# Hybrid decoder step: all row tiles of the down projection in the seven products, results by halves of the columns

## The chip, the cores and the metric

The kernel runs on one core of one Trainium2 chip. Its time is the device time of one execution in microseconds; the verdict compares it with the kernel before, run on the same chip. TensorE (PE, with PEld for its weight loads) multiplies, VectorE (DVE) and ScalarE (ACT) work element by element, GpSimd (POOL) issues some transfers and does a few additions, SyncE (SP) issues most transfers.

## The reference

One step of a two-layer decoder with 1024 prompt tokens and 8 sample tokens, 1032 columns in all, model width 1024 and MLP width 4096, in float32. Layer 0 mixes with gated linear attention, layer 1 with sliding-window attention; both attend to 256 memory tokens. What matters here is the MLP that ends each layer:

```python
def squared_relu_mlp(h, w_up, w_down):
    return jnp.square(jax.nn.relu(h @ w_up)) @ w_down

        f = squared_relu_mlp(rmsnorm(x, norm_ffn_pre[l]), w_ffn_up[l], w_ffn_down[l])
        x = x + rmsnorm(f, norm_ffn_post[l])
```

After layer 0, `x` is normalised again and goes through the K/V and query projections of layer 1. After layer 1, `x` is the output `yT`.

## The kernel before, in words

Activations lie with features on the 128 partitions and tokens in the columns. The 1032 columns are cut into three chunks `CH` of 384, 384 and 264. Every float32 product is made of three matmuls in a reduced type: each operand is split into a high part (a cast on ScalarE, L155) and a low part (a subtraction on VectorE, L156), and high x high, high x low and low x high are summed in PSUM.

The MLP's two projections are done as 2 x 2 block products with seven multiplications in place of eight (the Winograd form of Strassen's scheme). For the down projection the blocks are halves of the output features, halves of the MLP rows and halves of the columns (`HALF` = 516, worked in two parts of `SUB` = 258). The 32 row tiles of the MLP width are cut in two: the first four (`NPL`) are kept out of the scheme and done plainly, the other 28 go in pairs (`PAIRS`) through the seven products, with seven steps `jj` of four row tiles in each.

In the down projection `phases` lists the 49 steps (product, jj) in the order `ORDER` = 1, 7, 6, 5, 2, 3, 4. For each step `load_w` and `load_a` fetch the raw weights (`wr`) and the raw combined activations (`ra`, from the scratch tensor `awd`; three buffers), `prep` forms the product's combination and splits both, and `phase` issues 48 matmuls on eight PSUM banks. `prep` runs two steps ahead into three slots `sas` for the activations and three for the weights. With a product's last step `evict` adds the banks into the four quarter results `acc[11]`, `acc[12]`, `acc[21]`, `acc[22]`, as that product needs. Meanwhile in layer 0 `fold` multiplies layer 1's weights by a gain on GpSimd.

Then `down_plain` does the four plain row tiles chunk by chunk (96 matmuls each, L990 to L992), adds the quarter results to them (L996, L1000) into a tile `F`, and hands each pair of output tiles to `Residual`: squares and sums (`Stats`), a matmul with a constant matrix `ones` that averages over the partitions (L201), the inverse root by Ln and Exp with one Newton step (L208 to L212), then `f * rf`, the gain, the addition of the residual `xd`, and either the store of `xd` and the split for layer 1 (layer 0) or the store of `yT` (layer 1, L323 to L327). `measure` makes the statistics of the new `x`. A number given as `behind` puts the ones-matmul that many matmul columns later in TensorE's order. A scheduler orders each engine's instructions by priority and data; each engine and each queue then runs its list in order.

## Time and profile before

| | us |
|---|---|
| Median of 3 runs (2180.78 to 2186.23) | 2183.07 |
| The profiled execution, its own time | 2190.3 |
| Its span from first to last instruction | 2188.5 |
| TensorE busy in the span | 2143.8 (98%) |
| VectorE / ScalarE / GpSimd busy | 1492.9 / 1054.5 / 117.0 |
| Mean granted clock of TensorE | 0.993 |

The profile is of one execution; its times are used for the parts of the kernel, and differences are carried over to the median. A matmul's duration on the page covers its pipeline, so two neighbours overlap, and the pace is read from their starts. PE counts as busy when a matmul is in flight. On the other engines, an instruction's idle time before it is put down to what released it.

### The profile page before, as it was taken

To read this page: it belongs to the slowest core of one execution; us is meant where nothing else is said; L and a number is where in the kernel's file an instruction comes from. 1 tells how busy PE (TensorE), PEld (TensorE's weight loads), DVE (VectorE), ACT (ScalarE), POOL (GpSimd) and SP (SyncE) were. 2 spreads that over 40 slices of the span, in tenths; PEclk is the share of its full clock that TensorE was granted. 3 is DMA by queue.
4 is the path that set the end of the run, shared out by engine and by line. 5 is a ranking of instruction groups with operands and counts; after the bars stand their busy time and mean duration, and the time that the engine had idled before them with its cause. 6 is when DMAs were issued, how large, how long until landed. Compare 5 with 4: busy or idle time off the path is not lost.

```text
span 2188.5 us, 41306 instructions
## 1 busy us (share of the span) xinstructions
PE 2143.8 (98%) x16814; PEld 2047.8 (94%) x16814; DVE 1492.9 (68%) x2809; ACT 1054.5 (48%) x2095; POOL 117.0 (5%) x128
## 2 busy tenths in 40 slices
PE   8999999999999999999999999899999999999997
PEld 6879999899999999999999878599999999999996
DVE  7556647768877777657569455647887776856557
ACT  6355536557545544333424454646654554433334
POOL 0012000000000002520000000200000000000000
PEclk9999999999999999999999999899999999999998
DMA  5422026543653359474234200424364337635422
GB/s 169 143 67 77 24 65 169 154 136 103 194 174 135 134 199 360 165 262 135 93 94 148 91 19 24 164 89 135 117 213 160 137 132 274 213 110 172 150 89 78
DMA packets 122307, 304.73 MB, mean 139 GB/s; under 512 B 11065, under 2 KB 40817, under 8 KB 121761
## 3 DMA queue, kind: packets, MB, share of 16 engines
q1 hardware_dynamic: 109056, 258.80, 36.0%
q0 software_dynamic: 7728, 30.42, 4.0%
q10 hardware_dynamic: 5328, 12.81, 1.5%
q8 instruction: 134, 2.20, 0.4%
q14 instruction: 61, 0.50, 0.1%
HBM read 213.57 MB, written 89.51 MB: 138 GB/s over the span
## 4 chain that ended last, share of the span: by engine, by line
PE 90%; DVE 4%; ACT 3%; DMA 2%; issue 1%; SPq 0%; DVEq 0%; ACTq 0%
PE mm L251 17%; PE mx L251 8%; PE mx L760 6%; PE mx L762 6%; PE mx L761 6%; PE mx L925 4%; PE mx L927 4%; PE mx L926 4%; PE mm L762 3%; PE mm L760 3%; PE mm L761 3%; PE mm L925 2%; PE mm L926 2%; PE mm L927 2%; PE sx L925 1%; PE sf L926 1%
## 5 line engine op out<-in xcount | busy, mean ns | idle before, releaser
L155 ACT CAST wh<-ws 128x512 fp32r<-128x512 f32 (+1 forms) x262 | 188.3, 726 | 313.8 <-DVE ws L609 100.1
L760 PE MATMUL mx<-xf,wh 128*128 128x258 f32 x1048 | 296.9, 283 | 0.0
L762 PE MATMUL mx<-xf,wl 128*128 128x258 f32 x1048 | 295.7, 282 | 0.0
L761 PE MATMUL mx<-xf,wh 128*128 128x258 f32 x1048 | 295.5, 282 | 0.0
L156 DVE TENSOR_TENSOR wl<-ws,wh 128x512 fp32r<-128x512 f32 (+1 forms) x262 | 213.5, 821 | 105.2 <-ACT wh L155 103.9
L251 PE MATMUL mm<-xh,wh 128*128 128x384 f32 (+1 forms) x864 | 282.2, 327 | 0.5 <-ACT xh L155 0.4
L251 PE MATMUL mm<-xh,wl 128*128 128x384 f32 (+1 forms) x864 | 279.2, 323 | 0.0
L251 PE MATMUL mm<-xl,wh 128*128 128x384 f32 (+1 forms) x864 | 278.3, 322 | 0.0
L155 ACT CAST wh<-wr 128x1024 fp32r<-128x1024 f32 x98 | 103.0, 1051 | 319.3 <-PE sx L926 303.7
L156 DVE TENSOR_TENSOR wl<-wr,wh 128x1024 fp32r<-128x1024 f32 x98 | 119.8, 1223 | 175.9 <-ACT wh L155 175.9
L925 PE MATMUL mx<-sa,wh 128*128 128x258 f32 x784 | 221.2, 283 | 0.0
L926 PE MATMUL mx<-sa,wh 128*128 128x258 f32 x784 | 220.5, 281 | 0.0
L927 PE MATMUL mx<-sa,wl 128*128 128x258 f32 x784 | 220.4, 281 | 0.0
L761 PEld LDWEIGHTS mx<-xf,wh 128*128 128x128 f32 x1048 | 198.0, 189 | 0.4
L760 PEld LDWEIGHTS mx<-xf,wh 128*128 128x128 f32 x1048 | 197.6, 189 | 0.4
L762 PEld LDWEIGHTS mx<-xf,wl 128*128 128x128 f32 x1048 | 197.8, 189 | 0.0
L251 PEld LDWEIGHTS mm<-xh,wh 128*128 128x128 f32 x864 | 162.9, 189 | 10.4 <-issue 7.0
L251 PEld LDWEIGHTS mm<-xl,wh 128*128 128x128 f32 x864 | 162.9, 189 | 7.2 <-issue 6.3
L251 PEld LDWEIGHTS mm<-xh,wl 128*128 128x128 f32 x864 | 162.5, 188 | 6.8 <-issue 4.9
L926 PEld LDWEIGHTS mx<-sa,wh 128*128 128x128 f32 x784 | 148.3, 189 | 0.0
L927 PEld LDWEIGHTS mx<-sa,wl 128*128 128x128 f32 x784 | 148.0, 189 | 0.0
L925 PEld LDWEIGHTS mx<-sa,wh 128*128 128x128 f32 x784 | 147.4, 188 | 0.1
(560 smaller groups left out, 5782.8 us busy)
## 6 DMA issues: line engine op xcount, KB each, us to landing
ra<-awd SPq DMA_DIRECT2D x98, 516.0 KB, 3.6
ws<-in_w_up SPq DMA_DIRECT2D x64, 512.0 KB, 5.1
wr<-in_w_downb SPq DMA_DIRECT2D x56, 512.0 KB, 4.9
awd<-aw SPq DMA_DIRECT2D x26, 1032.0 KB, 6.7
awd<-am SPq DMA_DIRECT2D x28, 774.0 KB, 8.3
ws<-in_w_in_a SPq DMA_DIRECT2D x20, 512.0 KB, 3.9
xd<-f ACTq DMA_DIRECT2D x24, 384.0 KB, 4.7
ws<-in_w_out SPq DMA_DIRECT2D x16, 512.0 KB, 3.6
```

Of the source, the lines that this page charges most:

```text
L155: nc.scalar.copy(hi, src)
L156: (eng or nc.vector).tensor_tensor(lo, src, f32(hi), ALU.subtract)
L251: mm = nc.tensor.matmul(ps[:M, :n], w_[:, k, :M], x_[:, k, :], start=(i == 0), stop=(i == 3 * KT - 1))
L760: nc.tensor.matmul(ps, wh(k), xh, start=(k == 0), stop=False)
L761: nc.tensor.matmul(ps, wh(k), xl, start=False, stop=False)
L762: mm = nc.tensor.matmul(ps, wl(k), xh, start=False, stop=(k == n - 1))
L925: nc.tensor.matmul(ps, wh[:, q, ms], h, start=(jj == 0 and q == 0), stop=False)
L926: nc.tensor.matmul(ps, wh[:, q, ms], lo, start=False, stop=False)
L927: mm = nc.tensor.matmul(ps, wl[:, q, ms], h, start=False, stop=end)
```

## The change

The plain stage is gone. `NJ` = 8 steps in place of seven: the four plain row tiles of the up projection are still computed plainly, but now `plain_factors` forms their combinations in the up stage (eight subtractions or additions on VectorE, with loads and stores), and they enter the seven products as the step jj = 7. Three of the factors are read straight from `apd`. The order of the products becomes `DOWN` = 1, 7, 6, 4, 2, 5, 3, so that `acc[11]` and `acc[21]`, the left half of the columns, are complete after the fifth product, and `acc[22]` after the sixth; the seventh adds only to `acc[12]`.

The seventh product is done in two passes `s` over the two parts of 258 columns, 16 steps of 24 matmuls, with four banks in each pass. Its eight weight splits are kept for the second pass (`lasting`). The raw activations have two buffers in place of three, the halves of a fold take a temporary tile `t3`.

The result is not put together by chunks any more. `Closing` works on four pieces in place: `pa` (chunk 0, left columns 0 to 384), `pb` (132 columns of chunk 2), `pc` (258 columns of chunk 1) and `pd` (the other 126 of chunk 1 and the other 132 of chunk 2). `hook` places their steps among the phases: the squares of piece a four steps before the seventh product, the rest of pieces a and b from that product's start on, piece c in its second pass, and piece d after its end. The gain is multiplied on ScalarE for both layers. In layer 1 the residuals are fetched on GpSimd's queue into rooms of their own; in layer 0 they pass through `t3` on SP's queue.

The core of the diff (the eviction's rule by product, the pools and the tags of tiles are left out):

```diff
+DOWN = (1, 7, 6, 4, 2, 5, 3)
+NJ = DFF // P // 4
...
+        def plain_factors():
+            for q in range(2):
+                rows = [tp.tile([P, 768], F32, tag=tag, name=nm("c"))[:, :HALF] for tag in ("t3", "t3", "tq", "tq")]
+                for r, (m, h) in zip(rows, ((0, 0), (0, 1), (1, 0), (1, 1))):
+                    nc.sync.dma_start(r, apd[l, :, 2 * q + m, h, :])
+                c11, c12, c21, c22 = rows
+                for f_, r, a, b, op in ((1, c12, c22, c12, ALU.subtract), (4, c11, c12, c11, ALU.add),
+                                        (6, c21, c11, c21, ALU.subtract), (5, c22, c22, c11, ALU.subtract)):
+                    yield
+                    TT(r, a, b, op)
...
-        phases = [(p, jj) for p in range(7) for jj in range(NJ)]
+        phases = [(p, jj, None) for p in range(6) for jj in range(NJ)]
+        phases += [(6, jj, s) for s in range(2) for jj in range(NJ)]
+        N = len(phases)
...
-        rap = pool(st2, "left", "ra", 3)
+        rap = pool(st2, "left", "ra", 2)
...
+            order = [(q, mp) for q in range(2) for mp in range(4)]
+            if s is not None:
+                order.sort(key=lambda x: x[1])
+            for q, mp in order:
+                for x, (o, w) in enumerate(cols):
+                    ps = kept["ps"][len(cols) * mp + x][:, :w]
+                    ms = slice(P * mp, P * mp + P)
+                    a = 0 if s else o
+                    h, lo = sa[:, 0, q, a : a + w], sa[:, 1, q, a : a + w]
+                    end = jj == NJ - 1 and q == 1
+                    nc.tensor.matmul(ps, wh[:, q, ms], h, start=(jj == 0 and q == 0), stop=False)
+                    nc.tensor.matmul(ps, wh[:, q, ms], lo, start=False, stop=False)
+                    mm = nc.tensor.matmul(ps, wl[:, q, ms], h, start=False, stop=end)
+                    tick(mm, 3 * w)
+                    kept["mm"] = mm.ins.name
+                    if end:
+                        with first() if s is None else urgent(2):
+                            gather(DOWN[p], ps, *(acc[k][:, mp, o : o + w] for k in (11, 12, 21, 22)))
...
+        pa = piece(early, slice(0, 384), "sf", (0, 0, 384))
+        pb = piece(early, slice(384, HALF), "sx", (2, 0, 132))
+        pc = piece(late_, slice(0, SUB), "sf", (1, 0, SUB))
+        pd = piece(late_, slice(SUB, HALF), "sx", (1, SUB, 384 - SUB), (2, 132, 132))
...
+        def hook(v):
+            if -8 <= v < -4:
+                split(*lasting(v + 8), reg(3, v + 8))
+            if v == -4:
+                pa.feed(0, 1, 2, 3)
+            if v == 0:
+                rooms((pa, "xh0"), (pc, "xl0"))
+                pa.factor(rp.tile([P, 384], F32, tag="rf", name=nm("rf")), 0.3 * unit)
+            if v == 1:
+                pb.feed(0, 1, 2, 3)
+                pb.factor(rx, 2 * unit)
+            if v == 2:
+                pa.close(behind=kept["mm"])
+            if v == 4 and not l:
+                hl[0] = xtiles(0)
+                pa.cut(hl)
+            if v == 5:
+                rooms((pb, "xl2"))
+                pb.close(behind=kept["mm"])
+            if v == 7:
+                pc.feed(2, 3, 0, 1)
+                pc.factor(rb, 1.8 * unit)
+            if v == 9:
+                pc.close((2, 3, 0, 1), behind=kept["mm"])
+            if v == 11:
+                rooms((pd, "xh2"))
+            if v == 10 and not l:
+                rt[0] = rtile(0)
+                pa.measure(0, rt[0], 2.3 * unit, Ring())
+            if v == 11 and not l:
+                hl[1] = xtiles(1)
+                pc.cut(hl)
+                hl[2] = xtiles(2)
+                pb.cut(hl)
...
-        folds = dict(zip((21, 23, 25, 27, 35, 36, 38, 40, 41, 43, 45, 46), (2, 3, 0, 1, 10, 11, 4, 5, 6, 7, 8, 9)))
+        folds = dict(zip((2, 3, 4, 5, 6, 25, 26, 27, 28, 29, 36, 38), (2, 3, 0, 1, 10, 11, 4, 5, 6, 7, 8, 9)))
...
+        if l:
+            with urgent(2):
+                pd.finale()
+                pd.factor(rp.tile([P, 384], F32, tag="rf", name=nm("rf"))[:, : pd.n], 0)
+            pd.close()
```

The steps of `Closing`, which are new:

```python
        def feed(self, *pairs):
            for j in pairs:
                self.sf.add(self.f[:, 2 * j : 2 * j + 2, :])
                self.gain(2 * j, 2 * j + 1)
...
        def factor(self, rf, behind):
            self.rf = rf.unsqueeze(1).to_broadcast([P, 2, self.n])
            self.sf.finish(rf, behind)
...
            for i, j in enumerate(order):
                ks = slice(2 * j, 2 * j + 2)
                xs, fk = got[i], f[:, ks, :]
                TT(fk, fk, self.rf, ALU.mult)
                TT(fk, fk, xs, ALU.add)
...
        def cut(self, hl, order=(0, 1, 2, 3)):
            for j in order:
                ks = slice(2 * j, 2 * j + 2)
                for a, c, at in self.segs:
                    split(hl[c][0][:, ks, at], hl[c][1][:, ks, at], self.f[:, ks, :][:, :, a])
```

Three places show how the order moves. First, VectorE in the last product of layer 0. Before, these are the splits of weights (`wl<-wr`) and activations (`sa<-ra`) for the last steps, then those of the plain stage (`ah`, and `wl<-ws`):

```order
L156 TENSOR_TENSOR wl_10708<-wr_11431,wh_10707 128x1024
L156 TENSOR_TENSOR sa_10702<-ra_13329,sa_10702 128x1032
L156 TENSOR_TENSOR ah_13699<-t_1557_13700,ah_13699 128x768
L156 TENSOR_TENSOR ah_13699<-t_1558_13704,ah_13699 128x768
L156 TENSOR_TENSOR wl_10704<-wr_11616,wh_10703 128x1024
L156 TENSOR_TENSOR sa_10699<-ra_13383,sa_10699 128x1032
L156 TENSOR_TENSOR wl_13558<-ws_13555,wh_13557 128x1024
L156 TENSOR_TENSOR wl_13564<-ws_13561,wh_13563 128x1024
```

Now, in the first pass, the closing of piece a (`acc_10716` and `acc_10717`, with the factor `rf` and the residual tiles `t`), its cut (`xl<-acc`) and piece b's factor (`rx`) stand between the splits of the operands:

```order
L215 SCALAR_TENSOR_TENSOR rf_13696<-sf_13698,rf_13696 128x384
L158 TENSOR_TENSOR sa_10734<-ra_13761,sa_10734 128x2x258
L380 TENSOR_TENSOR acc_10716<-acc_10716,rf_13696 128x2x384 x2
L381 TENSOR_TENSOR acc_10716<-acc_10716,t_1572_13791 128x2x384
L158 TENSOR_TENSOR sa_10732<-ra_13811,sa_10732 128x2x258
L381 TENSOR_TENSOR acc_10716<-acc_10716,t_1573_13793 128x2x384
L380 TENSOR_TENSOR acc_10717<-acc_10717,rf_13696 128x2x384 x2
L158 TENSOR_TENSOR sa_10733<-ra_13841,sa_10733 128x2x258
L381 TENSOR_TENSOR acc_10717<-acc_10717,t_1574_13798 128x2x384
L213 TENSOR_TENSOR sx_13754<-sx_13754,rx_10742 128x132
L158 TENSOR_TENSOR xl_13872<-acc_10716,xh_13871 128x768
L214 SCALAR_TENSOR_TENSOR sx_13754<-sx_13754,rx_10742 128x132
```

A split of 2 x 258 elements is followed by two to five instructions of a piece before the next split comes.

Second, SP's queue in the same product. Before, it holds the loads of the activations, and those of the plain stage's factors (`t<-apd`):

```order
L878 DMA ra_13030<-awd 128x1032
L878 DMA ra_13085<-awd 128x1032
L967 DMA t_1557_13700<-apd 128x2x384
L967 DMA t_1558_13704<-apd 128x2x384
L878 DMA ra_13143<-awd 128x1032
```

Now the residual loads of pieces a, b and c (`t<-xd`) stand between the operand loads:

```order
L975 DMA ra_13881<-awd 128x2x258
L371 DMA t_1575_13803<-xd_94 128x768
L975 DMA ra_13931<-awd 128x2x258
L371 DMA t_1581_13911<-xd_96 128x2x132
L371 DMA t_1582_13913<-xd_96 128x2x132
L975 DMA ra_13959<-awd 128x2x258
L975 DMA ra_14019<-awd 128x2x258
L975 DMA ra_14051<-awd 128x2x258
L371 DMA t_1583_13918<-xd_96 128x2x132
L371 DMA t_1584_13923<-xd_96 128x2x132
L975 DMA ra_14099<-awd 128x2x258
L371 DMA t_1598_14079<-xd_95 128x2x258
```

What moved is the residual: before, its loads (`xs<-xd`) stood behind all operand loads.

Third, VectorE at the end of the program, in layer 1. Before, the statistics of chunk 2 (`f_24917`, factor `rf_25396`) and the closing of chunk 1 (`f_24913`, factor `rf_25229`) alternate:

```order
L1000 TENSOR_TENSOR f_24917<-mx_25378,acc_22020 128x132
L326 TENSOR_TENSOR f_24913<-f_24913,xall_25238 128x768
L323 TENSOR_TENSOR f_24913<-f_24913,rf_25229 128x768 x2
L210 TENSOR_TENSOR sf_25398<-sf_25398,rf_25396 128x264
L326 TENSOR_TENSOR f_24913<-f_24913,xall_25238 128x768
L211 SCALAR_TENSOR_TENSOR sf_25398<-sf_25398,rf_25396 128x264
L323 TENSOR_TENSOR f_24913<-f_24913,rf_25229 128x768
L212 SCALAR_TENSOR_TENSOR rf_25396<-sf_25398,rf_25396 128x264
L323 TENSOR_TENSOR f_24917<-f_24917,rf_25396 128x528 x2
L326 TENSOR_TENSOR f_24917<-f_24917,xall_25407 128x528 x2
L323 TENSOR_TENSOR f_24917<-f_24917,rf_25396 128x528 x2
```

Now the last addition of piece c (`xall_25145`) is followed by the last pass's evictions (L1031), and behind these stands piece d alone (factor `rf_25720`):

```order
L381 TENSOR_TENSOR acc_22258<-acc_22258,xall_25145 128x2x258
L1031 TENSOR_TENSOR acc_22258<-mm_25456,acc_22258 128x258
L1031 TENSOR_TENSOR acc_22258<-mm_25457,acc_22258 128x258
L1031 TENSOR_TENSOR acc_22258<-mx_25458,acc_22258 128x258
L192 TENSOR_TENSOR tq_25698<-tq_25698,tq_25709 128x516
L1031 TENSOR_TENSOR acc_22258<-mx_25459,acc_22258 128x258
L198 TENSOR_TENSOR rf_25720<-tq_25698 128x258
L213 TENSOR_TENSOR sx_25722<-sx_25722,rf_25720 128x258
L214 SCALAR_TENSOR_TENSOR sx_25722<-sx_25722,rf_25720 128x258
L215 SCALAR_TENSOR_TENSOR rf_25720<-sx_25722,rf_25720 128x258
L380 TENSOR_TENSOR acc_22258<-acc_22258,rf_25720 128x2x258 x2
L381 TENSOR_TENSOR acc_22258<-acc_22258,xall_25580 128x2x258 x2
```

No instruction of another piece is left between the factor's Newton steps (L213 to L215) and the last additions.

More of the change, by code (lines that the diff above doesn't have):

```diff
@@ L272, in feed @@
         def feed(self, m):
[L273 to L285 removed]
+            if m % 2:
@@ L315, in load @@
                 got.append(xs)
-            ahead = 4 if self.last else 2
-            for j in range(ahead):
-                load(j)
+            load(0)
+            load(1)
             for j in range(4):
@@ L342, in finish @@
-            return None if self.last else (hl, self.r)
-        def measure(self, behind, pool=None):
-            sx = Stats(self.n, "sx", pool)
-            for j in range(4):
-                sx.add(self.f[:, 2 * j : 2 * j + 2, :])
-            sx.finish(self.r, behind)
+                for k in (2 * j, 2 * j + 1):
+                    g = gains[:, self.gnext, k : k + 1]
+                    nc.scalar.mul(hl[0][:, k, :], f[:, k, :], g)
+                    STT(hl[1][:, k, :], f[:, k, :], g, f32(hl[0][:, k, :]), ALU.mult, ALU.subtract)
@@ L833, in mlp @@
                 square_mean(j - 2)
+            if i == ORDER[3] and j >= 5:
+                next(plain, None)
             if i == ORDER[-1]:
@@ L913, in phase @@
         def phase(t):
[L914 removed]
+            p, jj, s = phases[t]
+            cols = columns(t)
             wh, wl, sa = ready.pop(t)
             if jj == 0:
[L917 to L931 removed]
```

367 lines of the change are left out of this document (204 added, 163 removed).

## The prediction

> **What bounds the kernel now.** I read the page first, for the engine that carries the chain, then a table of windows over the MLP stages, then the timeline of TensorE for the pace of each shape, and last the end of the program.
>
> ```profile
> PE 2143.8 (98%) x16814; PEld 2047.8 (94%) x16814; DVE 1492.9 (68%) x2809; ACT 1054.5 (48%) x2095; POOL 117.0 (5%) x128
> PE 90%; DVE 4%; ACT 3%; DMA 2%; issue 1%; SPq 0%; DVEq 0%; ACTq 0%
> 540.00:822.00 282.00, 282.00 (x2349) 281.40 (x2348) 218.89 (x444) 144.84 (x259) 0.00 (x0) 1.00 0.49 167
> 822.00:1104.00 282.00, 282.00 (x2357) 281.97 (x2355) 181.99 (x199) 106.19 (x113) 62.69 (x36) 1.00 0.59 203
> 1104.00:1150.00 46.00, 46.00 (x295) 45.73 (x294) 34.78 (x65) 14.66 (x20) 0.00 (x0) 1.00 0.24 65
> 1150.00:1160.00 10.00, 10.00 (x59) 9.73 (x58) 9.88 (x15) 8.39 (x12) 0.00 (x0) 1.00 0.64 208
> 1842.00:2125.00 283.00, 283.00 (x2364) 282.96 (x2363) 176.25 (x201) 106.52 (x114) 6.37 (x12) 1.00 0.49 165
> 2125.00:2171.00 46.00, 46.00 (x291) 45.24 (x290) 32.85 (x62) 23.73 (x40) 0.00 (x0) 1.00 0.10 35
> 2171.00:2189.00 18.00, 1.85 (x7) 0.95 (x6) 13.57 (x18) 2.31 (x6) 4.09 (x2) 0.66 0.42 148
> ```
>
> The columns are the window, its length, the busy time of PE, PEld, DVE, ACT and POOL, the granted clock, the DMA share and GB/s. TensorE is 90% of the chain and has no idle time in the up stage (540 to 822), the seven down products (822 to 1104, 1842 to 2125), the plain stage (46 us in each layer) or the start of layer 1. The clock is 1.00 there. So a change inside these stages is worth what it does to the sum of matmul times, as long as the other engines stay ahead; after 2171 us TensorE is done and a tail of 17.5 us runs on VectorE.
>
> **The change part by part.** *Matmul time.* The plain stage issues 4 row tiles x 8 output tiles x 3 terms = 96 matmuls for each of three column chunks (384, 384, 264). It is replaced by an eighth step in each of seven products: 7 x 48 = 336 matmuls of 258 columns. The durations on the page overlap, so I take the pace from starts.
>
> ```profile
> L925 PE MATMUL mx<-sa,wh x392: 277/282/375, 822.5 to 1102.4; 128*128 128x258 f32 x196
> 1104.24 0.34 PE L990 MATMUL mm<-ah,wx 128*128 128x384 f32 x1
> 1127.81 0.33 PE L990 MATMUL mm<-ah,wx 128*128 128x384 f32 x1
> 1138.21 0.28 PE L990 MATMUL mx<-ah,wx 128*128 128x264 f32 x1
> 1148.50 0.28 PE L990 MATMUL mm<-ah,wx 128*128 128x264 f32 x1
> ```
>
> The products run from 822.5 to 1104.24: 7 x 7 x 48 = 2352 matmuls, 119.8 ns each. From 1127.81 to 1138.21 stand five output tiles of 12, 173 ns each at 384 columns; from there to 1148.50 seven of 12, 122.5 ns at 264. Plain: 192 x 0.1733 + 96 x 0.1225 = 45.0 us. New: 336 x 0.1198 = 40.3 us. That is -4.8 us a layer, **-9.6 us**. The two passes of the last product issue the same matmuls in another order. Each layer has one to four more small ones-matmuls for the statistics, since pieces are more than chunks: +0.3 us.
>
> Against it speaks a rule of the Trainium skill, Perfetto Trace Analysis, section Identifying the Most-Contended Engine: headroom on TensorE is judged by weight-load busy time. PEld is full in both stages, so by that rule time would follow the number of loads, 336 against 288. The starts above decide it for columns: two shapes, the same load, 119.8 against 173 ns.
>
> *The tail.* In layer 1 the last chunk's statistics share VectorE and GpSimd with chunk 1's closing.
>
> ```profile
> 2171.13 0.49 DVE L1000 TENSOR_TENSOR f<-mx,acc 128x132 f32<-128x132 f32 x2 [0.20 <-PE mx L992]
> 2173.31 0.42 ACT L209 ACTIVATE rf<-rf 128x264 f32<-128x264 f32 x1
> 2174.15 0.43 DVE L210 TENSOR_TENSOR sf<-sf,rf 128x264 f32<-128x264 f32 x1
> 2174.49 2.21 DVE L326 TENSOR_TENSOR f<-f,xall 128x768 f32<-128x768 f32 x1
> 2176.97 0.94 DVE L323 TENSOR_TENSOR f<-f,rf 128x768 f32<-128x768 f32 x1
> 2177.84 0.42 DVE L212 SCALAR_TENSOR_TENSOR rf<-sf,rf 128x264 f32<-128x264 f32 x1
> 2178.04 1.80 POOL L326 TENSOR_TENSOR f<-f,xall 128x768 f32<-128x768 f32 x1 [2.15 <-issue]
> 2178.29 2.74 DVE L323 TENSOR_TENSOR f<-f,rf 128x528 f32<-128x528 f32 x2
> 2180.95 1.31 DVE L326 TENSOR_TENSOR f<-f,xall 128x528 f32<-128x528 f32 x2
> L327 SPq DMA_DIRECT2D out_yT<-f x12: 372/372/378, 2152.5 to 2184.8; - x12
> out_yT<-f SPq DMA_DIRECT2D x4, 264.0 KB, 2.2
> ```
>
> After the change nothing else is queued there: the order has piece c closed before the last evictions, and no GpSimd add. The Exp ends at 2173.73; three dependent Newton steps of 0.45 (2177.84 to 2178.29) end at 2175.1 in place of 2178.29, -3.2. The first pair of multiplications took 2.66 to the next start beside GpSimd, a pair without it 1.31, -1.4. The last piece goes out in two DMAs a pair of rows, one more issue of 0.37. Tail: **-4.2 us**; bounds 0 (piece c still in line) and -4.6 (the issue hidden). One rule speaks against: the Trainium skill, DMA: Bandwidth & Descriptors, section Specifications, has transfers under 512 B as read-modify-write. The stores of 126 columns have rows of 504 B. No run here shows that price; if it doubled the landing, the tail would gain 2.0 instead.
>
> *VectorE in the last product.* This is the term I trust least. The closing of pieces a, b and c moves between the operand splits on which TensorE waits, and a pass step has only 24 matmuls, 2.88 us.
>
> ```profile
> L598 DVE TENSOR_TENSOR acc<-acc,sx 128x258 f32<-128x258 f32 x1 | 0.4, 424 | 0.0
> L156 DVE TENSOR_TENSOR ah<-t,ah 128x528 fp32r<-128x528 f32 x2 | 1.3, 703 | 0.2 <-ACT ah L155 0.2
> L189 DVE TENSOR_TENSOR tq<-tq,tq 128x768 f32<-128x768 f32 x6 | 5.7, 952 | 2.7 <-ACT tq L183 2.7
> L156 DVE TENSOR_TENSOR wl<-wr,wh 128x1024 fp32r<-128x1024 f32 x2 | 2.5, 1225 | 5.0 <-ACT wh L155 5.0
> 943.00 0.41 DVE L588 TENSOR_TENSOR acc<-mx,acc 128x258 f32<-128x258 f32 x1
> 943.33 0.41 DVE L589 TENSOR_TENSOR acc<-mx,acc 128x258 f32<-128x258 f32 x1
> ```
>
> In layer 0, counted in the order from the sixth product's first eviction to the last split: 20 evictions and 22 other small operations at 0.424, 14 operand splits and 11 operations of 516 columns at 0.70, one weight split of 1.2, 15 operations of 768 columns (closing, cutting and measuring piece a) at 0.952. Sum 50.8 us. Back to back each starts 0.08 before the last one's end (943.00 to 943.33), 83 x 0.08 = 6.6, so 44.2. Available: 2.5 us before the product's end and 15 steps, 45.7. Layer 1 has no cut and no measure, 37.7. So layer 0 fits with 1.5 us to spare, while it also waits for ScalarE and for TensorE's slots; I take +2 there and +0.5 in layer 1, bounds 0 and 7. Two in-order queues are part of that: layer 0's residual stores stand on ScalarE's queue and wait for VectorE's additions, with the casts of the next operands behind them; the residual loads stand on SP's queue and wait for a temporary tile that an addition frees, with the operand loads behind them. In the order each of these waits is for work that stands ahead of the split that the blocked load or cast serves, so I give them no term of their own.
>
> *The join of the layers.* Plain stage and first projections ran with VectorE at 9.88 of 10 us and TensorE never idle. Piece d now ends with TensorE and must be normalised and cut while chunk 0's six projections run: 6 x 24 x 0.1733 = 25.0 us. VectorE's list from the last eviction to the last cut sums to 26.5 us by the same durations, some 22 overlapped. Chunk 1's first matmul is due at about 26.7 us with the transposes and ones-matmuls. +1, bounds 0 and 6.
>
> *What I cost at nothing.* The eight combinations of the plain rows in the up stage (8 x 0.70 us) lie under 282 us of TensorE with VectorE at 218.89; without cover 5.6 us a layer. The folds run by halves on GpSimd:
>
> ```profile
> L240 POOL TENSOR_TENSOR wf<-wf,gains 128x1024 f32<-128x1024 f32 x12 | 49.1, 4094 | 65.0 <-DMA wf<-in_w_in_b 37.1 <-DMA wf<-in_w_kv 27.8
> ```
>
> Their products are needed 200 us later, and five now fall into the first product, where DMA is busiest. Two raw buffers in place of three matter only where loads are slow; that is a rival.
>
> **Sum**: -9.6 - 4.2 + 0.3 + 2.5 + 1.0 = -10.0 us. The profiled execution took 2190.3 us (span 2188.5), 7.2 above the median of the runs, and would take 2180.3; on the median of 2183.07 that is **2173.1 us**. About 0.3% (6.5 us) is what a measurement here can tell from no change.
>
> **The rivals.**
>
> *Loads bound the last product (slower).* With two raw buffers a load is issued only when the split two steps before is done.
>
> ```profile
> ra<-awd SPq DMA_DIRECT2D x7, 516.0 KB, 6.4
> ra<-awd SPq DMA_DIRECT2D x9, 516.0 KB, 3.6
> L155 ACT CAST ah<-t 128x528 fp32r<-128x528 f32 x2 | 1.2, 628 | 0.0
> 815.00:860.00 45.00, 45.00 (x379) 45.00 (x378) 32.09 (x31) 21.62 (x25) 8.73 (x8) 1.00 0.98 366
> ```
>
> The cycle is issue 0.37 + landing + cast 0.63 + split 0.70 for two steps of TensorE, 5.75 us: it decides from a landing of 4.05 us on. At 3.6 us (900 to 950, half busy) it is hidden; at the 6.4 us of 815 to 860, where DMA is 98% busy, each pair of steps loses 2.35, eight pairs 18.8, less some 4.3 of lead: 14.5 a layer. 2173.1 - 2.5 + 29 = **2200 us**. For it: residual loads, stores and layer 1's weights pass the same queue between these loads. Against: 16 operand loads of 258 KB, three residual pieces in and out (774 columns, 3.2 MB each way) and five weight tiles of 512 KB are 13 MB in 46 us, 285 GB/s, under the 366 of that window, and each load is half as large. Slower by 0.3% needs a landing of 5.7. 11%.
>
> *VectorE bounds the last product.* If its operations do not overlap (50.8 against 45.7, 5.1) and it stands idle once for a chain of Square, ones-matmul, Ln and Exp (from 2171.6 to 2173.7 in the tail, 2.1), 7.2 in place of 2.5: **2178 us**, no change. For it: the list is in order, and each chain of a piece leaves the engine and comes back. Against: most chains have splits and other pieces' work queued in between. 12%.
>
> *Chunk 1 waits for piece d.* The order lets piece d's sums wait for the evictions of chunk 0's projections, so its list cannot run ahead of TensorE; 26.5 us without overlap, the chain of 2.1 and a last load of 3.6 behind weights on SP, less 26.7, is 5.5, the whole bound of 6 in place of 1: **2178 us**, no change. Against: before, VectorE was as full there and nothing waited. 7%.
>
> *Weight loads set the pace.* PEld is full in every stage (281.97 of 282, 45.73 of 46). If the number of loads counted, 45.0 x 336/288 = 52.5, +7.5 a layer in place of -4.8: 2173.1 + 24.6 = **2198 us**. The starts of 119.8 and 173 ns behind one and the same load refute it. It is also what the rule on weight-load time would make of the change. 2%.
>
> **How the numbers follow.** Forecast 68%, all of it faster. The second and third rival, 19%, are within 0.3%; the first and fourth, 13%, slower. The range takes in the forecast's bounds, from no stalls and the scatter of the runs (2.7 below their median), 2173.1 - 3.5 - 0.4 - 2.2 = 2167, to the two middle rivals with scatter, 2182. It leaves out the slow rivals and little else.
>
> **What would show it.** Right: each layer's seven products take some 322 us (2688 x 0.1198) and TensorE is idle in them for under 3 us; layer 1's projections start directly behind; from the last matmul to the end pass 13 us, with VectorE's Newton steps back to back. Wrong: TensorE waiting for the operand splits step after step in the last product (VectorE named: second rival; DMA named, landings over 4 us: first), or for the cut at chunk 1 of layer 1's first projections.

## The result, and the profile after

The changed kernel took 2213.26 us (median of 4 runs, 2209.3 to 2217.6) against 2184.52 for the kernel before (2180.78 to 2186.23, on the same chip): the ratio is 1.0134, 95% interval 1.0122 to 1.0146. It is slower by 28.7 us, where 10 us less were forecast. The profiled execution took 2217.6 us, span 2215.8.

The parts of the span, from the first matmul of the seven up products to the first of the down products, from there to the last down matmul, and so on (differences of the first and last starts at those lines, each from one profiled execution):

| us | up, layer 0 | down, layer 0 | attention, layer 1 | up, layer 1 | down, layer 1 | after the last matmul |
|---|---|---|---|---|---|---|
| before | 283.4 | 327.3 | 409.5 | 283.4 | 328.1 | 17.7 |
| after | 307.8 | 330.5 | 411.5 | 286.3 | 328.7 | 14.4 |

The largest loss, 24.4 us, lies in layer 0's up stage, where the prediction had costed everything at nothing. The down stages, which should have won 2.5 and 4 us, won nothing. Only the tail came out on the forecast's side. From the page of after, the busy shares and the chain; TensorE fell from 90% of the chain to 61%, and loads of `ws` stand on it now:

```profile
PE 2144.0 (97%) x16918; PEld 2042.9 (92%) x16918; DVE 1505.1 (68%) x2839; ACT 1083.0 (49%) x2191; POOL 111.4 (5%) x170
PE 61%; DVE 16%; DMA 13%; ACT 6%; issue 4%; SPq 0%; ACTq 0%; POOL 0%; DVEq 0%
```

The windows of after that answer to the first two shown of before (same columns):

```profile
540.00:822.00 282.00, 265.54 (x2154) 260.89 (x2153) 212.11 (x415) 127.67 (x230) 54.17 (x72) 0.99 0.63 203
844.00:1124.00 280.00, 277.30 (x2300) 276.17 (x2301) 182.84 (x200) 120.11 (x142) 0.00 (x0) 0.99 0.48 157
```

TensorE did 2154 matmuls in 282 us where it had done 2349. GpSimd, idle in the up stage before, is busy for 54.17 us there and not at all in the down products: the folds run in the wrong stage. GpSimd's timeline of after shows the first of them:

```profile
645.69 0.58 POOL L244 DMA_DIRECT2D t<-in_w_kv  x1 [306.34 <-ACT aw L851]
...
652.06 1.05 POOL L246 TENSOR_TENSOR t<-t,gains 128x512 f32<-128x512 f32 x1
653.41 0.59 POOL L247 DMA_DIRECT2D wfd<-t  x1 [0.30 <-POOL t L246]
```

The fold's load starts when ScalarE has done with the temporary tile (`aw L851`), over 200 us before the matmul behind which it was put. TensorE's waits in that stage (line waited for: us, times, longest):

```profile
PE mx L818 <- DVE aw L647: 9.5, 8, 2.3
PE mm L818 <- DVE aw L647: 4.0, 3, 3.5
PE mm L818 <- DVE aw L644: 1.6, 2, 1.1
```

L644 and L647 are evictions of up products on VectorE. Before, TensorE waited for none of them.

### The profile page after: what moved, and what is told of

It reads as the page before. It is cut to its first block, busy times and chain, and to the rows that moved or that the text cites. A ratio compares the mean times of both kernels' runs of the same rounds, so it can differ in the third digit from the quotient of the medians.

```text
span 2215.8 us, 41850 instructions
## 1 busy us (share of the span) xinstructions
PE 2144.0 (97%) x16918; PEld 2042.9 (92%) x16918; DVE 1505.1 (68%) x2839; ACT 1083.0 (49%) x2191; POOL 111.4 (5%) x170
## 4 chain that ended last, share of the span: by engine, by line
PE 61%; DVE 16%; DMA 13%; ACT 6%; issue 4%; SPq 0%; ACTq 0%; POOL 0%; DVEq 0%
PE mm L257 13%; DMA ws<-in_w_up 7%; PE mx L257 6%; PE mx L1049 5%; PE mx L1050 5%; PE mx L1051 5%; DVE wl L158 4%; PE mm L1049 2%; PE mm L1050 2%; PE mm L1051 2%; ACT wh L157 1%; DMA ra<-awd 1%; DMA t<-xd 1%; PE mx L818 1%; PE mx L819 1%
## 5 line engine op out<-in xcount | busy, mean ns | idle before, releaser
L158 DVE TENSOR_TENSOR wl<-wr,wh 128x1024 fp32r<-128x1024 f32 x102 | 124.9, 1224 | 180.3 <-ACT wh L157 179.8
L1049 PE MATMUL mx<-sa,wh 128*128 128x258 f32 x840 | 239.7, 285 | 4.3 <-DVE aw L651 1.9
L1050 PE MATMUL mx<-sa,wh 128*128 128x258 f32 x840 | 237.3, 283 | 1.6 <-DVE sa L158 1.6
L1051 PE MATMUL mx<-sa,wl 128*128 128x258 f32 x840 | 237.0, 282 | 0.0
L1049 PEld LDWEIGHTS mx<-sa,wh 128*128 128x128 f32 x840 | 160.0, 190 | 6.0 <-DVE aw L651 2.4
L1050 PEld LDWEIGHTS mx<-sa,wh 128*128 128x128 f32 x840 | 159.9, 190 | 2.2 <-DVE sa L158 2.0
L1051 PEld LDWEIGHTS mx<-sa,wl 128*128 128x128 f32 x840 | 159.5, 190 | 0.0
```

The source lines that it names most:

```text
L158: (eng or nc.vector).tensor_tensor(lo, src, f32(hi), ALU.subtract)
L1049: nc.tensor.matmul(ps, wh[:, q, ms], h, start=(jj == 0 and q == 0), stop=False)
L1050: nc.tensor.matmul(ps, wh[:, q, ms], lo, start=False, stop=False)
L1051: mm = nc.tensor.matmul(ps, wl[:, q, ms], h, start=False, stop=end)
```

## The experiments

The 18 runs and their times, each beside runs of the kernel before on its chip:

| run | what it is | median us (range) | ratio to before, 95% interval |
|---|---|---|---|
| e1_folds_held | after, folds really wait | 2194.3 (2190.5 to 2196.2) | 1.0038 [1.0026, 1.0051] |
| e2_folds_dma_only | after, folds without multiplication | 2199.3 (2198.7 to 2205.9) | 1.0060 [1.0043, 1.0077] |
| e3_folds_mult_only | after, folds without transfers | 2202.1 (2200.3 to 2206.3) | 1.0075 [1.0056, 1.0094] |
| e4_before_new_folds | before, with the new folds | 2202.4 (2201.7 to 2210.0) | 1.0074 [1.0057, 1.0091] |
| e5_plain_rows_gpsimd_queue | e1, plain rows on GpSimd's queue | 2203.1 (2200.5 to 2208.9) | 1.0087 [1.0062, 1.0111] |
| e7_no_plain_rows | e1, no combinations of plain rows | 2190.0 (2180.4 to 2197.2) | 1.0020 [1.0003, 1.0037] |
| e8_raw_loads_first | e1, two loads swapped | 2195.0 (2188.1 to 2198.6) | 1.0043 [1.0032, 1.0055] |
| b1_plain_rows_in_down | e1, combinations in the down stage | 2189.9 (2185.7 to 2196.2) | 1.0025 [1.0013, 1.0037] |
| e9_before_two_raw | before, two raw buffers | 2182.1 (2177.8 to 2188.9) | 0.9993 [0.9981, 1.0006] |
| e10_before_extra_vector | before, 5.6 us more VectorE work | 2185.0 (2182.3 to 2188.1) | 1.0004 [0.9994, 1.0013] |
| b2_loads_in_order | b1, weight loads in order of use | 2188.1 (2182.4 to 2194.6) | 1.0020 [1.0009, 1.0032] |
| e11_before_stride | before, factor array of 8 steps | 2197.3 (2194.9 to 2200.8) | 1.0060 [1.0044, 1.0076] |
| a1_after_old_stride | after, 7 steps and an array of its own | 2197.8 (2188.5 to 2205.1) | 1.0062 [1.0040, 1.0084] |
| e1s_held_old_stride | e1, the same | 2178.3 (2171.8 to 2183.9) | 0.9976 [0.9965, 0.9987] |
| b5_best_old_stride | b2, the same | 2178.6 (2174.8 to 2182.2) | 0.9972 [0.9963, 0.9982] |
| s9_before_nine_steps | before, factor array of 9 steps | 2183.9 (2180.4 to 2192.9) | 1.0007 [0.9996, 1.0018] |
| s16_before_sixteen_steps | before, factor array of 16 steps | 2188.6 (2185.2 to 2191.1) | 1.0019 [1.0009, 1.0029] |
| e1p_held_nine_steps | e1, factor array of 9 steps | 2177.1 (2171.5 to 2184.0) | 0.9969 [0.9957, 0.9980] |

The runs lie on several chips, on which the kernel before took 2183.5 to 2184.9 us. Differences below are of medians; taken from the ratios they come out up to 3 us smaller or larger, and a difference of 1 or 2 us between two runs is not shown. Stage times are of one profiled execution each.

**The folds.** The first theory was that they run ahead because a dependency without synchronisation orders the scheduler's list only: it puts nothing between two engines, and GpSimd's list held nothing else in that place. The edit of e1:

```diff
-            tc.add_manual_dep(d.ins, behind, NOSYNC, reason="behind later matmuls")
+            tc.add_manual_dep(d.ins, behind, mybir.DependencyInfo(mybir.DependencyClass.Sync, ...), ...)
```

> The changed kernel with one edit: each fold's load really waits for the matmul it is put behind (a synchronising dependency in place of one that only orders the schedule). Theory A (the folds run ahead, in layer 0's up stage, and cost it): no GpSimd work between 540 and 820 us, the up stage of layer 0 takes some 286 us as layer 1's does, not 307.8, and the time falls by 20 to 24 us, to 2189 to 2193. Theory B (the combinations of the plain rows, whose loads and stores now stand on SP's queue between the weight loads, cost it, and the folds only happen beside): the up stage stays over 300 us and the time within 4 us of 2213.

e4 puts the new `fold` alone into the kernel before, in place of the old one and its buffer:

```diff
-                fold(folds.pop(t), wfp)
+                fold(folds.pop(t), kept["mm"])
```

> The kernel before with one part of the change: the folds by halves in the temporaries of the up stage, ordered behind matmuls by the schedule alone; the plain stage, the three raw buffers and the old closing stay. Theory A: the folds run ahead here too, and the kernel before loses some 20 us in layer 0's up stage, 2200 to 2207. Theory B (plain rows on SP's queue, which this kernel doesn't have): 2182 to 2187, no difference.

Holding the folds took 18.9 us off the changed kernel, to 1.3 above the range expected, and the new folds alone put 17.9 on the kernel before. Theory A holds, in both directions. What in them costs was asked by halves. In `fold`:

```diff
# e2
-            nc.gpsimd.tensor_tensor(ws, ws, gains[:, g, ks]..., ALU.mult)
# e3
-            d = nc.gpsimd.dma_start(ws, src[:, ks, :])
+            d = nc.gpsimd.tensor_tensor(ws, gb, gb, ALU.mult)
...
-            nc.gpsimd.tensor_tensor(ws, ws, gains[:, g, ks]..., ALU.mult)
-            nc.gpsimd.dma_start(wfd[i][:, ks, :], ws)
```

> The changed kernel, the folds still ahead, without GpSimd's multiplication (24 fewer instructions); it leaves out the gains of layer 1's K/V and W_in weights. If the traffic of the folds costs the up stage (24 loads and 24 stores of 256 KB), layer 0's up stage stays at 300 to 308 us and the time at 2206 to 2213. If GpSimd's multiplications cost it (VectorE slowed beside them), the up stage falls to some 286 us and the time to 2190 to 2194. Theory B of the held folds: no difference in either case, 2209 to 2217.

> The mirror image: the folds' 24 multiplications alone, ahead as before, on the gains and without any load or store; layer 1 reads its K/V and W_in weights without their gains. They stand back to back (some 24 x 1.5 = 36 us of GpSimd from about 645 us). If the multiplications cost the up stage: over 300 us, time 2206 to 2213. If the traffic does: up stage some 286 us, time 2190 to 2194. Theory B: 2209 to 2217.

Both fell between their cases: the transfers alone cost 5.0 us over e1, the multiplications alone 7.7, and together 18.9. The expectation that one of them carries it was wrong, and 6.2 us arise only with both; how is not shown. The multiplications slow VectorE, for whose evictions TensorE waits (L644 and L647 above). Groups of VectorE, 640 to 700 us (busy, mean ns of one), first e1, then e3:

```profile
L158 DVE TENSOR_TENSOR wl<-ws,wh 128x512 fp32r<-128x512 f32 x20 | 13.6, 687 | 8.5 <-ACT wh L157 8.5
```

```profile
L158 DVE TENSOR_TENSOR wl<-ws,wh 128x512 fp32r<-128x512 f32 x19 | 16.7, 890 | 5.6 <-ACT wh L157 5.6
```

The same split takes 687 ns without GpSimd beside it and 890 on average in e3, where the 24 multiplications stand close together (642.5 to 679.7 us). A single pair in the timeline of after, rows of VectorE and GpSimd:

```profile
692.80 0.69 DVE L158 TENSOR_TENSOR wl<-ws,wh 128x512 fp32r<-128x512 f32 x1
694.36 1.24 POOL L246 TENSOR_TENSOR t<-t,gains 128x512 f32<-128x512 f32 x1 [1.14 <-DMA t<-in_w_in_b]
694.61 1.53 DVE L158 TENSOR_TENSOR wl<-ws,wh 128x512 fp32r<-128x512 f32 x1
...
696.40 0.41 DVE L641 TENSOR_TENSOR aw<-mx,aw 128x258 f32<-128x258 f32 x1
696.54 1.03 POOL L246 TENSOR_TENSOR t<-t,gains 128x512 f32<-128x512 f32 x1
```

The split that meets a multiplication takes 1.53 in place of 0.69; the eviction from PSUM (`mx`) that overlaps the next one keeps its 0.41. The Trainium skill, SBUF — State Buffer, section Terms, says that VectorE and GpSimd share a pair of ports that one of them locks for a whole instruction; the 0.84 us more agree with that.

**What was left with the folds held.** e1 was still 9.9 us over the kernel before: 6.0 in layer 0's up stage (289.4), 1.0 in layer 1's, and both layers' down products began badly. The 49th matmul of the products starts 6.9 us (layer 0) and 6.1 us (layer 1) later than 48 matmuls at 0.1198 us would have it; in the kernel before it is on time, and in the changed kernel 5.8 and 7.0 us late. ScalarE, VectorE and TensorE at that place in layer 1, rows picked from the timeline of e1:

```profile
1848.82 1.05 ACT L157 CAST sa<-ra 128x1032 fp32r<-128x1032 f32 x1 [4.32 <-DMA ra<-awd]
1849.91 1.23 DVE L158 TENSOR_TENSOR sa<-ra,sa 128x1032 fp32r<-128x1032 f32 x1 [4.51 <-ACT sa L157]
1851.06 0.42 DVE L651 TENSOR_TENSOR aw<-mm,aw 128x258 f32<-128x258 f32 x1
1853.00 0.47 PE L1049 MATMUL mx<-sa,wh 128*128 128x258 f32 x1 [1.30 <-DVE aw L651]
1855.28 0.42 PE L1049 MATMUL mm<-sa,wh 128*128 128x258 f32 x1
1855.50 0.42 PE L1050 MATMUL mm<-sa,wh 128*128 128x258 f32 x1
```

The first raw operand lands late, ScalarE and VectorE wait for it with the up stage's last evictions (L651, L653) queued behind, and TensorE waits for these. What follows runs at half pace: 0.22 us from start to start in place of 0.12. The profile gives the reason, a granted clock of 0.50 (the first number behind GpSimd's), in a window of e1:

```profile
1853.10:1859.90 6.80, 6.03 (x25) 5.44 (x26) 6.80 (x10) 4.31 (x6) 0.00 (x0) 0.50 1.00 390
```

Three suspects: the plain rows' loads and stores on SP's queue (Q), their VectorE work (V), the two raw buffers and the place of the loads (R).

```diff
# e5: in plain_factors, the loads and stores
-                    nc.sync.dma_start(...)
+                    nc.gpsimd.dma_start(...)
# e7: plain_factors is never run, four products read the first step's rows as their eighth
-            if i == ORDER[3] and j >= 5:
-                next(plain, None)
# e8: for the first three steps
-                load_w(t)
                 load_a(t)
+                load_w(t)
# b1: as e7, but run in the loop over the down phases; five folds move into the second product
+            if 3 <= t < 12:
+                next(plain, None)
```

> The kernel with the held folds, and the loads and stores of the plain rows' combinations moved from SP's queue to GpSimd's; the eight VectorE operations of a layer stay. The held folds left three losses: layer 0's up stage 6 us over the kernel before, layer 1's 1 us, and some 6 us at the start of each layer's down products, where evictions stand on VectorE behind a split that waits for the first raw operand. Theory Q (SP's queue: the plain rows' loads and stores hold up the weight loads behind them): most of this goes, 2180 to 2185. Theory V (VectorE's own loop of weight load, cast, split and eviction has hardly any slack in the up stage, and the combinations use it up): it stays, 2190 to 2196. Theory R (two raw buffers and the place of the first raw loads alone cause the stall at the start): up stage as in V, 2190 to 2196.

> The kernel with the held folds, without the combinations of the plain rows (no loads, operations or stores of them in the up stage; the eighth step of four products reads the first step's rows in their place). Theories Q and V: up stages at 283 to 285 us in both layers and the stall at the start of the down products gone or under 2 us, 2176 to 2182. Theory R: the up stages recover 5 us, the stall stays, 2187 to 2190.

> The kernel with the held folds, with one swap: for the first three steps of the down products the raw operand's load stands ahead of the weight load on SP's queue, so that it does not wait for the weight buffers that VectorE's last up-stage splits free. Up stages unchanged (289 and 284 us). Theories V and R: the first raw operand lands 4 us or more earlier and most of the 6 us at the start of each layer's products goes, 2183 to 2188. If the stall has another cause (VectorE late with the evictions themselves): 2191 to 2196.

> A version meant to beat both: folds held and five of them moved into the second product, and the combinations of the plain rows moved from the up stage into steps 7 to 14 of the down products, where VectorE is busy for about 13 of 20 us. Theories Q and V: as without the plain rows, 2176 to 2182, if nothing in the first two products waits for the loads and stores that come on top there (8 loads and 8 stores of 258 KB a layer). If these now delay the operand loads: 2183 to 2190.

e5 was slower than either theory had it. Its waits in layer 1's up stage, of TensorE and of VectorE:

```profile
PE mx L818 <- DVE aw L644: 6.1, 1, 6.1
```

```profile
DVE c L878 <- DMA c<-apd: 6.3, 1, 6.3
```

The combinations stand in VectorE's list ahead of evictions; their loads now came later, VectorE waited 6.3 us once, and TensorE with it. With that one wait, and a granted clock of 0.50 for some 6.8 us about its end, the stage was 8.1 us longer than in e1. In e7 and b1 the up stages came to 284 to 286 us, but the stall at the start of the down products stayed, and the time stopped at 2190. For e7 that is what theory R had (2187 to 2190); Q and V fell short, since even without any plain row the losses did not go. e8 told nothing on R: the scheduler left the first raw load behind the factor stores, where it had been. The next three took R, V and the order of the loads alone:

```diff
# e9, in the kernel before
-        rap = pool(st2, "left", "ra", 3)
+        rap = pool(st2, "left", "ra", 2)
# e10, in the kernel before, in eight of the pairs
+            if i == ORDER[3] and 4 <= j < 12:
+                gb = gains[:, 0, 0:1].to_broadcast([P, HALF])
...
+                    TT(tp.tile([P, 768], F32, tag="t3", name=nm("c"))[:, :HALF], gb, gb, ALU.mult)
# b2: in load_w; made[1] is the last matmul of the up stage
+                if t > 1 and s is None:
+                    tc.add_manual_dep(d.ins, kept["mm"] if t > 7 else made[1], mybir.DependencyInfo(mybir.DependencyClass.Sync, ...), ...)
```

> The kernel before with one number changed: two buffers for the raw operands of the down products in place of three. Theory R (two buffers change what stands on SP's queue around the first raw load, a weight load for a much later step now follows directly and shares the bandwidth, and the first operand lands late): each layer's down products start with some 5 us of waits and half-pace matmuls, 2190 to 2196. Theory L (the first load is late because VectorE and ScalarE come some 2 to 3 us late out of the up stage in the kernels with the change, whatever the buffers): 2183 to 2187, no difference.

> The kernel before with eight more VectorE operations of 516 columns in each layer's up stage (5.6 us, on the gains into a temporary that nobody reads): the work of the plain rows' combinations without their loads, stores and waits. Theory V (VectorE's in-order loop of weight load, cast, split and eviction runs at nearly TensorE's pace although VectorE is busy for only 219 of 282 us; what pushes it behind stays behind to the end of the stage and makes the first down operands late): up stages 2 to 5 us longer, a stall at the start of the down products, 2189 to 2198. If the 63 idle us are free: 2183 to 2187.

> The version with the plain rows in the down products, and its weight loads kept in the order of use: those of steps 2 to 7 wait for the last matmul of the up stage, those of later steps for the step six before, so that the first two raw operands have the DMA engines to themselves. If the shared bandwidth makes the first operand late (theory R, as far as it goes by loads): the first raw load lands in about 6.5 us in place of 9.4 to 9.7, the stall at the start of each layer's products is under 2 us, 2178 to 2184. If VectorE's lag alone makes it late: 2187 to 2192.

Two buffers cost nothing, and 5.6 us of VectorE work cost nothing (up stages of 283.4 in both). b2 came out 1.8 us under b1, which is not clear of the scatter: with the weight loads out of the way its first raw load still landed in 9.5 us (layer 0) and 9.2 us (layer 1). So V is out, and of R the two buffers by themselves and the traffic of the weight loads. What delayed both stages seemed to be none of the instructions in them.

**The factor array.** What still differed in the up stage was seen in the transfers (KB each, us from issue to landing): first before, then e11, at 650 to 815 us.

```profile
awd<-aw SPq DMA_DIRECT2D x8, 1032.0 KB, 6.8
ws<-in_w_up SPq DMA_DIRECT2D x14, 512.0 KB, 6.6
awd<-am SPq DMA_DIRECT2D x8, 774.0 KB, 8.6
ra<-awd SPq DMA_DIRECT2D x3, 516.0 KB, 7.8
```

```profile
awd<-aw SPq DMA_DIRECT2D x8, 1032.0 KB, 7.5
ws<-in_w_up SPq DMA_DIRECT2D x14, 512.0 KB, 7.5
awd<-am SPq DMA_DIRECT2D x8, 774.0 KB, 9.3
ra<-awd SPq DMA_DIRECT2D x3, 516.0 KB, 9.9
```

The last row is the first loads of the down products. The store of a pair's first four factors takes 7.4 to 7.5 us in e1, e7, b1 and b2 too. It is one transfer to four places of `awd`, and the change made that DRAM array one step longer: `[2, 7, NJ, P, 2, HALF]` with 8 steps of 516 KB in place of 7. The distance from factor to factor went from 3612 to 4128 KB.

```diff
# e11, in the kernel before
-    awd = dram.tile([2, 7, len(PAIRS) // 2, P, 2, HALF], ...)
+    awd = dram.tile([2, 7, len(PAIRS) // 2 + 1, P, 2, HALF], ...)
# a1, e1s, b5: the eighth step's rows apart, stored to `awe` and loaded from it
-    awd = dram.tile([2, 7, NJ, P, 2, HALF], ...)
+    awd = dram.tile([2, 7, NJ - 1, P, 2, HALF], ...)
+    awe = dram.tile([2, 7, P, 2, HALF], ...)
```

> The kernel before with the factor array in DRAM one step longer (its eighth step is never written or read): the stride between the seven factors grows from 3612 to 4128 KB, all else is equal. Theory D (the larger stride makes the stores of the factors, and the weight loads between them, slower): the factor store of 1032 KB lands in 7.4 us or more in place of 6.7, VectorE waits longer for the weights, the up stages take 284 to 288 us and the down products start late, 2187 to 2195. Otherwise 2182 to 2186, no difference.

> The changed kernel with one edit: the eighth step's rows lie in an array of their own, so that the factors keep the old stride of 3612 KB. The folds still run ahead. Theory D: it recovers what the stride costs beside the folds, 2195 to 2206. Otherwise 2210 to 2216.

> The kernel with the held folds and the old stride; the combinations of the plain rows stay in the up stage. Theory D: up stages within 1 us of the kernel before, most of the stall at the start of the down products gone, 2178 to 2187. Otherwise 2191 to 2197.

> The best version so far (folds held, plain rows in the down products, weight loads in order of use) with the old stride. Theory D: up stages at 283.4 us in every run, 2176 to 2182, faster than both kernels. Otherwise as it was, 2185 to 2191.

Theory D holds in all four; e11 came out 2.3 us above its range. The stride alone puts 13.8 us on the kernel before, by the path seen in e1: VectorE waits longer for the weight loads between the stores (the waits of VectorE in layer 0's up stage, before and e11; 25.3 in e1 and 14.9 in e1s),

```profile
DVE ws L609 <- DMA ws<-in_w_up: 17.6, 12, 2.6
```

```profile
DVE ws L609 <- DMA ws<-in_w_up: 24.1, 11, 3.2
DVE sa L156 <- ACT sa L155: 5.8, 1, 5.8
```

it comes late to the end of the stage, and the first operand of the down products comes late too. Most of the loss stands there: in e11 the up stage of layer 0 is 3.2 us longer, and the 49th matmul of the products is 7.8 us late in layer 0 and 3.8 in layer 1; after it nothing more is lost to the end of the seven products. In e1s the 49th matmul is late by 0.0 and 1.4. Taking the stride away is worth 15.5 us to the changed kernel, 16.1 to e1 and 9.5 to b2, in which the weight loads already stand apart. With both causes gone the time is 2178.3, 35.0 under the changed kernel; one by one they were worth 18.9 and 15.5. The last runs ask which strides; the array gets 9 or 16 steps, of which the last are never used:

```diff
# s9 and s16, in the kernel before
+    awd = dram.tile([2, 7, 9, P, 2, HALF], ...)
+    awd = dram.tile([2, 7, 16, P, 2, HALF], ...)
# e1p, in e1
+    awd = dram.tile([2, 7, NJ + 1, P, 2, HALF], ...)
```

> The kernel before with the factor array allocated for nine steps (stride between the factors 4644 KB, neither the 3612 of before nor the 4128 of the change); steps 8 and 9 are never used. If a stride close to a multiple of 4096 KB is what makes the four rows of a factor store collide: 2182 to 2187 and the 1032 KB store lands in 6.7 us. If a longer array or stride as such does it: 2195 to 2200, 7.5 us or more.

> The kernel before with the factor array allocated for sixteen steps (stride 8256 KB, again close to a multiple of 4096 KB). Collision at multiples of 4096 KB: as with eight steps, 2193 to 2200, the store lands in 7.4 us or more. If only 4128 itself is bad: 2182 to 2187.

> The kernel with the held folds and one more number changed: the factor array padded to nine steps, with no array of its own for the eighth. Collision at 4096 KB: as with the old stride, 2176 to 2182. Length as such: 2192 to 2200.

A longer array costs nothing at 4644 KB, and e1p, two small edits of the changed kernel, is 0.31% under the kernel before. It, e1s and b5 are equal within their scatter, and faster than both kernels by intervals that leave out 1. 8256 KB costs some 4.7 us, less than was expected; its store lands in 7.0 to 7.3 us, and the 49th matmul is late by 1.0 and 4.8. That a distance a little over a multiple of 4096 KB is what hurts fits the four strides (3612 and 4644 free, 4128 dear, 8256 in between); why is not shown. The size of the array by itself is not it: 9 steps cost nothing, nor do the 7 and 1 of e1s. Where the arrays lie in memory was not recorded. The Trainium skill, DMA: Bandwidth & Descriptors, section Latency and other measured facts, reports copies at half their rate when the row pitch is 4 or 8 MiB, and at the full rate with 4 KiB more. Here 32 KB more than 4 MB, between the factors and not between rows, were not enough; for such a store the measurement decides.

## Why the prediction was wrong, step by step

**Failed: what was costed at nothing.** "Their products are needed 200 us later, and five now fall into the first product, where DMA is busiest." None fell there. The place in the code was taken for the place in time; all 24 halves ran from 652 to 770 us, in layer 0's up stage, for which the prediction had asked only whether the eight combinations were covered. That step is worth 18 to 20 us. Held where they were meant to run (853 to 1063 us in e1), the folds cost nothing that shows: in e1s TensorE has a single wait in layer 0's down stage, and it is for something else.

**Failed: a line of the change that had no step.** The working has no word on the longer `awd`. It is worth 14 to 17 us in the kernel before, the changed one and e1. Neither it nor the folds was among the rivals with a chance, and the range ended at 2182.

**Right: the matmul time.** Without the two disturbances the seven products take 2688 x 0.1198 = 322.0 us and the stages come close to it. Windows of e1s, the up and down stages of both layers:

```profile
535.00:818.00 283.00, 283.00 (x2357) 282.40 (x2356) 226.55 (x455) 146.69 (x260) 0.00 (x0) 1.00 0.52 179
818.00:1140.00 322.00, 319.88 (x2674) 319.07 (x2673) 231.89 (x272) 145.44 (x189) 63.51 (x72) 1.00 0.60 199
1553.00:1836.00 283.00, 283.00 (x2358) 282.40 (x2357) 222.99 (x452) 145.49 (x260) 0.00 (x0) 1.00 0.52 177
1836.00:2158.00 322.00, 321.03 (x2687) 320.37 (x2686) 216.81 (x268) 136.17 (x175) 13.50 (x20) 1.00 0.50 163
```

The down stages of e1s take 324.8 and 323.1 us, of the kernel before 327.3 and 328.1. The up stages are at 283.4 with the plain rows' combinations in them: that "nothing" was right, as e10 says for their VectorE work. The rival of the weight loads' pace is refuted by these times, and that of loads bounding the last product by TensorE's waits in e1s: none there is for an operand. In the kernel before, two raw buffers cost nothing (e9).

**Right in size, only in part in mechanism, the last product.** +2 in layer 0 and +0.5 in layer 1 were taken, for operand splits that come late; in e1s layer 0 waits 2.1 us once, in a ones-matmul for piece c's sums on VectorE, and layer 1 not once. No split came late, so that the sizes agree is in part luck. **Too small, the join.** +1 was taken. TensorE's waits in e1s from 1140 to 1180 us sum to 4.2:

```profile
PE sx L205 <- DVE rf L199: 2.7, 1, 2.7
PE sT L258 <- ACT xh L158: 0.8, 1, 0.8
PE sf L1847 <- DVE tq L193: 0.4, 1, 0.4
PE mm L258 <- DVE acc L1032: 0.3, 1, 0.3
```

The 2.7 are piece d's ones-matmul, which waits in TensorE's order for VectorE's sum; that is near the third rival's mechanism, a few us large. **Too large, the tail.** -4.2 was taken, -3.3 came (17.7 to 14.4). Rows from the end of before, then of after:

```profile
2170.51 0.42 DVE L195 TENSOR_TENSOR rf<-tq 128x264 f32<-128x264 f32 x1
2170.98 0.71 PE L201 MATMUL sf<-rf,ones 128*128 128x264 f32 x2
2171.53 1.32 PE L201 MATMUL sf<-t,ones 128*128 128x264 f32 x4
```

```profile
2202.01 0.42 DVE L1031 TENSOR_TENSOR acc<-mx,acc 128x258 f32<-128x258 f32 x1
2202.35 0.42 DVE L198 TENSOR_TENSOR rf<-tq 128x258 f32<-128x258 f32 x1
2202.82 0.70 PE L204 MATMUL sx<-rf,ones 128*128 128x258 f32 x2 [1.16 <-DVE rf L198]
2203.36 1.03 PE L204 MATMUL sx<-t,ones 128*128 128x258 f32 x4
2204.85 0.42 ACT L212 ACTIVATE rf<-rf 128x258 f32<-128x258 f32 x1
2205.30 0.43 DVE L213 TENSOR_TENSOR sx<-sx,rf 128x258 f32<-128x258 f32 x1 [2.53 <-ACT rf L212]
2206.24 0.43 DVE L215 SCALAR_TENSOR_TENSOR rf<-sx,rf 128x258 f32<-128x258 f32 x1
```

The Newton steps do run back to back, as forecast. The working kept the end of the Exp where it was. But the sum of the squares (`rf`), which before was formed ahead of the last matmul's start at 2170.8, now stands behind the last eviction (L1031) in VectorE's list, as the order ahead of the prediction shows. So the six ones-matmuls of the mean begin 1.4 us after the last matmul's start at 2201.4, before 0.2, and the Exp ends 3.9 us after it, before 2.9 (2170.8 to 2173.73). The doubled landing of stores with rows of 504 B, which the working weighed, did not come: the 126 columns landed in 2.0 us, as did the 132 columns in e1s; before, 264 took 2.2. With 3.2 us of error in the join and 0.9 in the tail, the forecast's -10.0 becomes some -6; e1s, the change without its two accidents, measures -5.2, and e1p -6.9, so that their medians lie 4 to 5 us above the 2173.1 that was forecast.

## What to carry to other kernels

A dependency that orders only the schedule holds no engine back: work put "behind" another engine's instruction starts when its own queue and its buffers let it, so look in the trace when it runs, and make it wait where that matters. When a scratch array in DRAM grows, work out the distance between places that one transfer writes together, and try a padded one: a step more of unused memory was worth some 15 to 17 us here (e1 to e1p). Before costing work at nothing beside a busy engine, ask which in-order lists wait for its loads; 5.6 us of bare work cost nothing, one late load in front of evictions cost 8 (e5).

## What the runs showed of the hardware

- In the kernel before, one transfer of 1032 KB to four places landed in 6.6 to 6.8 us with 3612 or 4644 KB between them, in 7.2 to 7.5 with 4128 KB (e11), in 7.0 to 7.3 with 8256 KB (s16); the weight loads beside it took 6.6, 7.5 and 6.8 us in layer 0 (before, e11, s16).
- A VectorE subtraction of 512 columns took 0.69 us alone and 1.53 beside a GpSimd multiplication of the same size; an eviction of 258 columns from PSUM kept its 0.41 (after).
- Right behind waits of 0.39 and 1.30 us, TensorE's granted clock was 0.50 from 1853.1 to 1859.9 us in e1, and matmuls of 258 columns started 0.22 us apart in place of 0.12. In e5 it was 0.50 from 1651.7 to 1658.5, about the end of a wait of 6.1 us (to 1652.8).
